# Hybrid encoder layer on one core: sums of w_ada row by row across the chunk ahead, in two alternating sums, and late transposes of x moved back

## The chip, the core and the metric

The program runs on one core of a Trainium2 chip. Five engines work side by side, each through its own queue in order: TensorE (PE: matmuls and transposes into PSUM), VectorE (DVE) and ScalarE (ACT) for elementwise work, GpSimd (POOL), and SyncE (SP), which here issues nearly all DMAs. The metric is the device time of one execution in microseconds (us), lower is better.

## What is computed

```
mod = silu(c) @ w_ada + b_ada                       # c: (1, 2048), w_ada: (2048, 3 * 2048)
shift, scale, gate = split(mod, 3)
h = rms_norm(x, g) * (1 + scale) + shift            # x: (1, 512, 2048)
q_a, k_a, v_a, z_a, q_r, k_r, v_r, z_r = split(h @ w_in)   # w_in: (2048, 7168)
y_a = dilated_attention_mixture(q_a, k_a, v_a)      # 8 heads of 128
y_r = bidirectional_retention(q_r, k_r, v_r)        # 4 heads
out = concat(y_a * silu(z_a), y_r * silu(z_r)) @ w_out     # w_out: (2048, 2048)
result = rms_norm(x + gate * out, final_gain)
```

All is float32. The change lies in how shift and scale are made and turned into h, ahead of the product with w_in.

## The kernel before

The 2048 columns of x and h are 16 blocks of 128, turned so that the block stands on the partitions: `xT[k]` is block k of the normalised x, 128 x 512. Each block of h is kept as a high part `hh[k]` and a low part `hl[k]` in fp32r, each piece of a weight likewise as two halves of a tile `w`, and a product is three matmuls (`mm3`): high x high, high x low, low x high.

The first part of the product with w_in goes through 13 **units** (256 columns of w_in each: q, k, v, z of the head pairs, `ph1`), but not block by block for one unit at a time: it goes by **chunks** of blocks, `CHUNKS = [1, 2, 2, 3, 4, 4]`. Chunk 0 is block 0, chunk 1 blocks 1 and 2, chunk 2 blocks 3 and 4, chunk 3 blocks 5 to 7, chunk 4 blocks 8 to 11, chunk 5 blocks 12 to 15. In each chunk all 13 units are multiplied with that chunk's blocks. So PE can begin with block 0 while shift and scale of the later blocks are still being made. Two units keep their sums in PSUM (`pp`), the others have their partial products in banks `pw` (three banks in turn), which ACT copies (chunk 0) or DVE adds (later) into tiles `acc0` to `acc12` in SBUF. In chunk 2 five of these go by ACT into tiles `more` instead and are added later.

A unit's piece of weights is loaded (`raw`), ACT casts its high half (L180), DVE subtracts to get the low half (L185), and PE multiplies. Three tiles `w` are in use in turn, so ACT's cast for a piece waits until PE has done the piece three before.

Beside that run, for each chunk ahead, the pieces made by `ada_pieces`: loads of the shift and scale columns of w_ada for the chunk's blocks (`araw`, three buffers; one holds 4, 4, 2, 2, 2 rows of blocks for chunks 1 to 5), and for each of the 16 blocks of rows one operation that multiplies it with the block's column of silu(c) and adds it into `aacc` (the first is an ACT activation at L239, the other 15 are DVE operations at L243, 512, 512, 768, 1024 and 1024 wide). Then `sums`: the sum of `aacc` over the partitions, for chunk 1 by matmuls with a column of ones (L257), for the others by transposes into the one bank of the pool `psM` (`psm`, L273), which ACT reads with accumulation (L278); for chunks 3 and later in two halves, one bank each in turn. Three small DVE operations make `sv` and `av`. Last `h_pieces`: ACT makes `hh` and `ht` (for chunk 1 DVE makes `ht`), DVE subtracts to get `hl` (L211).

What sets the order: the main loop feeds the units' pieces as **items**. An item is loaded when it is fed, converted `lead` items later (2 in chunk 0, 8 from then on) and multiplied two items after that. A table `agenda` holds what is to be called after which item: `plan` lays the pieces for the next chunk evenly over the items of the present one, from the third on, and the last quarter of x (row tile 3: transposes L380 and copies L391) after items 10 to 13. Since the items are loaded ten ahead of their matmuls, what is called at an item stands ahead of matmuls of ten items earlier. A scheduler then sets the final order of each engine by what it takes to be ready, except where `pin` keeps the order; `after` adds an order between two instructions without a semaphore.

Of the kernel before, what the change touches and what calls it, by code (L numbers as in the profile page):

```python
# [55 lines left out]
def trunk_kernel(ctx, tc, x, c, norm_gain, w_ada, b_ada, w_in, w_out, dec_f, dec_b, final_gain, out):  # L56
# [116 lines left out]
    def conv(src, n, at, pin_low=None):  # L173
# [7 lines left out]
        if pin_low is not None:  # L181
            pin_low.append(lambda: pin(nc.vector.tensor_tensor(dl, src, f32(dh), op=ALU.subtract)))
# [35 lines left out]
    def ada_pieces(k0, nk):  # L218
# [16 lines left out]
        def add(kr):  # L235
            rv = raws[kr]
            for a in range(npc):
                if kr + a == 0:
                    first = nc.scalar.activation(acc[:, :, :n], rv[:, a], AF.Copy, scale=ct[:, 0:1])  # L239
                    if k0 in (1, 3):  # L240
                        after(first, marks["hh"])
                else:
# [4 lines left out]
                    if k0 in (1, 3) and kr + a == 1:
                        after(ins, marks["hl"])

        def sums():  # L250
            ks = slice(k0, k0 + nk)
            sl = slice(NK + k0, NK + k0 + nk)
            if k0 == 1:
                ps = bank(psM, "psm")
                for b in range(2):
                    for j in range(nk):
                        nc.tensor.matmul(  # L257
                            ps[:, b * nk + j : b * nk + j + 1], acc[:, b, j * P : (j + 1) * P], ones[:, 0:1],
                            start=b + j == 0, stop=b + j == nk, skip_group_check=True,
                        )  # L260
# [1 line left out]
                nc.vector.tensor_tensor(av[:, ks], ps[:, nk : 2 * nk], bg[:, sl], op=ALU.add)
                marks["hl"] = nc.vector.tensor_tensor(
                    av[:, ks], av[:, ks], bg[:, 32 + k0 : 32 + k0 + nk], op=ALU.mult
                )
# [1118 lines left out]
```

## Time and profile before

| | us |
|---|---|
| median of 3 runs (lowest, highest) | 940.17 (938.87, 942.82) |
| the profiled execution | 940.26 |
| its span, first to last instruction | 938.5 |
| PE busy in it | 920.0 |
| DVE busy | 619.9 |
| ACT busy | 381.0 |
| mean granted TensorE clock | 0.997 |

The span is that of the instructions; 1.8 us of the execution's time lie around it. Busy time of PE is the union of the matmuls as they are shown, and these overlap: a matmul is shown for longer than it holds up the next one. So a stretch is judged by the number of its matmuls and by their step from start to start. A digit of the slices stands for 23.5 us, a fortieth of the span.

### The profile page before, as it was taken

The numbers are of one execution on the slowest core, as the hardware profiler recorded it, in microseconds if no ns is written. First come the engines' busy times: TensorE is split into PE (matmuls) and PEld (weight loads), VectorE is DVE, ScalarE is ACT, GpSimd is POOL, SyncE is SP. The second block draws the span as 40 slices with busy tenths as digits, with TensorE's granted clock in tenths as the row PEclk, the third lists the DMA queues.
The fourth block names the chain that finished last, engine by engine and source line by source line (L and its number), as shares of the span: only waits on it lengthen the run. The fifth ranks groups of instructions, "written<-read, shape, count | busy, mean of one in ns | idle before, by whom it ended". The sixth has DMA issues, their size and how long they took to land.

```text
span 938.5 us, 14336 instructions
## 1 busy us (share of the span) xinstructions
PE 920.0 (98%) x5578; PEld 807.9 (86%) x5578; DVE 619.9 (66%) x1096; ACT 381.0 (41%) x752; POOL 13.7 (1%) x25
## 2 busy tenths in 40 slices
PE   8999999999999999999999999999999999999996
PEld 5787788888988888988998899998899988888896
DVE  4899999959467886666675565845744382546554
ACT  4843525253254655444343232422343372324321
POOL 2000000000000000000000000000000000000001
PEclk9999999999999999999999999999999999999998
DMA  9987988524322222214444534434513148234305
GB/s 329 352 294 259 308 288 281 177 90 127 100 90 67 70 67 70 66 55 136 149 134 146 179 102 158 144 126 158 167 58 112 65 162 290 90 130 140 111 3 180
DMA packets 110244, 141.50 MB, mean 151 GB/s; under 512 B 5800, under 2 KB 81496, under 8 KB 109792
## 3 DMA queue, kind: packets, MB, share of 16 engines
q1 hardware_dynamic: 109072, 137.27, 44.6%
q10 hardware_dynamic: 1008, 3.28, 0.9%
q8 instruction: 44, 0.72, 0.3%
q14 instruction: 24, 0.20, 0.1%
q0 software_dynamic: 96, 0.03, 0.0%
HBM read 136.36 MB, written 4.20 MB: 150 GB/s over the span
## 4 chain that ended last, share of the span: by engine, by line
PE 84%; DVE 7%; DMA 4%; issue 2%; ACT 2%; POOL 0%; SPq 0%; POOLq 0%; DVEq 0%; ACTq 0%
PE pp L97 24%; PE pw L97 12%; PE pp L95 12%; PE po L97 12%; PE pw L95 6%; PE po L95 6%; DVE aacc L243 3%; PE op L97 3%; DMA araw<-in_w_ada_dram 2%; PE sp L97 2%; PE op L95 2%; PE tp L799 1%; DMA raw<-in_w_ada_dram 1%; DVE w L185 1%; PE sp L95 1%
## 5 line engine op out<-in xcount | busy, mean ns | idle before, releaser
L185 DVE TENSOR_TENSOR w<-raw,w 128x512 fp32r<-128x512 f32 (+1 forms) x288 | 193.6, 673 | 214.8 <-ACT w L180 214.5
L180 ACT CAST w<-raw 128x512 fp32r<-128x512 f32 (+1 forms) x289 | 174.7, 606 | 390.5 <-PE pp L97 187.1
L95 PE MATMUL pp<-w,hh 128*128 128x256 f32 x576 | 160.2, 278 | 0.0
L97 PE MATMUL pp<-w,hh 128*128 128x256 f32 x576 | 159.7, 277 | 0.0
L97 PE MATMUL pp<-w,hl 128*128 128x256 f32 x576 | 159.7, 277 | 0.0
L95 PEld LDWEIGHTS pp<-w,hh 128*128 128x128 f32 x576 | 108.4, 188 | 1.0 <-issue 0.2
L97 PEld LDWEIGHTS pp<-w,hh 128*128 128x128 f32 x576 | 108.3, 188 | 0.9
L97 PEld LDWEIGHTS pp<-w,hl 128*128 128x128 f32 x576 | 108.2, 188 | 0.0
L95 PE MATMUL pw<-hh,w 128*128 128x512 f32 x256 | 101.5, 397 | 3.4 <-DVE acc L994 2.1
L95 PE MATMUL pp<-hh,w 128*128 128x512 f32 x256 | 99.8, 392 | 0.4 <-DVE kl L699 0.4
L97 PE MATMUL pw<-hh,w 128*128 128x512 f32 x256 | 100.0, 391 | 0.1
L97 PE MATMUL pp<-hl,w 128*128 128x512 f32 x256 | 100.0, 391 | 0.0
L97 PE MATMUL pp<-hh,w 128*128 128x512 f32 x256 | 99.9, 390 | 0.0
L97 PE MATMUL pw<-hl,w 128*128 128x512 f32 x256 | 99.7, 391 | 0.0
L97 PE MATMUL po<-w,yh 128*128 128x512 f32 (+1 forms) x252 | 91.1, 361 | 0.0
L95 PE MATMUL po<-w,yh 128*128 128x512 f32 (+1 forms) x252 | 91.0, 361 | 0.0
L97 PE MATMUL po<-w,yl 128*128 128x512 f32 (+1 forms) x252 | 91.0, 361 | 0.0
L243 DVE SCALAR_TENSOR_TENSOR aacc<-araw,ct,aacc 128x512 f32<-128x512 f32 (+2 forms) x75 | 76.4, 1018 | 5.6 <-DMA araw<-in_w_ada_dram 2.9
L994 DVE TENSOR_TENSOR acc<-acc,pw 128x512 f32<-128x512 f32 x95 | 63.5, 686 | 4.6 <-PE pw L97 4.1
L95 PEld LDWEIGHTS pw<-hh,w 128*128 128x128 f32 x256 | 48.1, 188 | 17.2 <-DVE acc L994 4.7
L95 PEld LDWEIGHTS pp<-hh,w 128*128 128x128 f32 x256 | 48.0, 188 | 10.8 <-DVE kl L699 0.8
L97 PEld LDWEIGHTS pw<-hh,w 128*128 128x128 f32 x256 | 48.1, 188 | 10.6 <-DVE w L185 0.5
(237 smaller groups left out, 1568.6 us busy)
## 6 DMA issues: line engine op xcount, KB each, us to landing
raw<-in_w_in_dram SPq DMA_DIRECT2D x94, 512.0 KB, 3.6
araw<-in_w_ada_dram SPq DMA_DIRECT2D x48, 512.0 KB, 6.8
graw<-in_w_ada_dram SPq DMA_DIRECT2D x64, 256.0 KB, 3.0
raw<-in_w_out_dram SPq DMA_DIRECT2D x32, 512.0 KB, 3.7
raw<-in_w_in_dram SPq DMA_DIRECT2D x16, 384.0 KB, 4.1
araw<-in_w_ada_dram SPq DMA_DIRECT2D x16, 384.0 KB, 4.3
res<-in_x_dram SPq DMA_DIRECT2D x16, 256.0 KB, 6.2
raw<-in_w_in_dram SPq DMA_DIRECT2D x11, 256.0 KB, 5.1
```

The costliest lines, as they stand in the source:

```text
L95: nc.tensor.matmul(o, lh, rh, start=start, stop=False, skip_group_check=True)
L97: nc.tensor.matmul(o, a, b, start=False, stop=stop and b is (rl if swap else rh), skip_group_check=True)
L180: c1 = nc.scalar.copy(dh, src)
L185: c2 = nc.vector.tensor_tensor(dl, src, f32(dh), op=ALU.subtract)
L243: ins = nc.vector.scalar_tensor_tensor(acc[:, :, :n], rv[:, a], ct[:, kr + a : kr + a + 1], acc[:, :, :n], op0=ALU.mult, op1=ALU.add,)
L799: nc.tensor.transpose(tp_[:, j * P : (j + 1) * P], pt[:, j * P : (j + 1) * P], ident)
L994: nc.vector.tensor_tensor(accs[u][i], accs[u][i], ps[i], op=ALU.add)
```

## The change

Line numbers move by 2 to 42; the rows of the changed order carry the new ones (cast L182, low half L191, row add L254, transposed sums L290, reading L295, `hh` L203, `ht` L208, `hl` L217, add into `acc` L1033).

- The rows of w_ada are added one by one as separate pieces (`row`), not four or two in a piece. For chunks 2, 3 and 4 they are laid over the first 0.78, 0.78 and 0.62 of the items of the chunk before, counted from where PE is (`fed + LEAD1 + LOOK`) and not from where the loads are; the sums follow 0.04 of the items later and the making of h is spread up to 0.92, 0.92 and 0.78. Chunk 1 has places of its own in a table, chunk 5 is laid as before.
- For chunks 1 and 2 even and odd rows go into two sums, both begun by ACT. For chunk 1 the column matmuls take both sums (eight instead of four), for chunk 2 one DVE operation joins them ahead of the transposes. For chunk 1 `av` is made by one operation for each block, ahead of `sv`.
- Each row's add has an order after a conversion (`marks`).
- The last quarter of x is turned after items 10, 23, 25 and 27, and ACT alone copies it to `xT`.
- The larger lead of 8 begins two items later.

```diff
+LATE = 10, 23, 25, 27
+FIRST_AT = 3, 4, 5, 6, 8, 10, 13, 14, 15, 15, 16, 16
...
+        two = 2 * n <= 4 * P
+        part = [acc[:, :, :n], acc[:, :, n : 2 * n]] if two else [acc[:, :, :n]]
...
-        def add(kr):
+        def add(kr, only=None):
             rv = raws[kr]
-            for a in range(npc):
-                if kr + a == 0:
-                    first = nc.scalar.activation(acc[:, :, :n], rv[:, a], AF.Copy, scale=ct[:, 0:1])
+            for a in range(npc) if only is None else [only]:
+                r = kr + a
+                s = part[r % len(part)]
+                if r < len(part):
+                    first = nc.scalar.activation(s, rv[:, a], AF.Copy, scale=ct[:, r : r + 1])
...
+                    after(ins, marks["split" if k0 == 1 else "prev"])
...
+            if two:
+                nc.vector.tensor_tensor(part[0], part[0], part[1], op=ALU.add)
...
+        def row(r):
+            add(krs[r // npc], r % npc)
+            if r % npc == npc - 1 and r // npc + AR < len(krs):
+                load(krs[r // npc + AR])
...
+        if ends:
+            n_items, rows_end, h_end = ends
+            at = [i - 5 for i in range(AR)] + [r * rows_end * n_items / NK - 0.5 for r in range(NK)]
...
+            s = (rows_end + 0.04) * n_items
+            at += [s] + [s + 0.3 + (h_end * n_items - s) * j / len(hs) for j in range(len(hs))]
+            return list(zip(at, fs + [sums] + hs))
...
-        evacuated(3, b, dve if b else act, True)
+        evacuated(3, b, act, True)
...
+        if fed == NU + LEAD0:
+            early["lead"] = LEAD1
...
+            ends = {1: (0.78, 0.92), 2: (0.78, 0.92), 3: (0.62, 0.78)}.get(ci)
...
+            if ci == 0 or ends:
+                for at, f in nxt:
+                    agenda.setdefault(at if ci == 0 else fed + LEAD1 + LOOK + math.floor(at), []).append(f)
+            else:
+                plan(nxt, fed + LAG, span)
```

What this does to the order of the instructions, at the places that the prediction speaks of:

DVE, around the low halves `hl3` of chunk 2's blocks 3 and 4, in before (`w` are conversions of weights, `acc` the units' sums, `aacc` the sum of rows of w_ada, here that of chunk 3, 768 wide):

```order
L185 TENSOR_TENSOR w_866<-raw_637,w_866 128x512
L994 TENSOR_TENSOR acc11_0_365<-acc11_0_365,pw_869 128x512
L243 SCALAR_TENSOR_TENSOR aacc_750<-araw_860,ct_142,aacc_750 128x2x384
L994 TENSOR_TENSOR acc11_1_366<-acc11_1_366,pw_870 128x512
L211 TENSOR_TENSOR hl3_784<-ht_715,hh3_79 128x512
L211 TENSOR_TENSOR hl3_784<-ht_747,hh4_80 128x512
L185 TENSOR_TENSOR w_890<-raw1_665,w_890 128x512
L994 TENSOR_TENSOR acc4_0_351<-acc4_0_351,pw_893 128x512
L994 TENSOR_TENSOR acc4_1_352<-acc4_1_352,pw_894 128x512
L243 SCALAR_TENSOR_TENSOR aacc_750<-araw_863,ct_142,aacc_750 128x2x384
L185 TENSOR_TENSOR w_921<-raw_698,w_921 128x512
```

The same place in the changed order:

```order
L299 TENSOR_TENSOR av_144<-av_144,bg_147 128x2
L1033 TENSOR_TENSOR acc5_1_354<-acc5_1_354,pw_954 128x512
L217 TENSOR_TENSOR hl3_972<-ht_942,hh3_79 128x512
L217 TENSOR_TENSOR hl3_972<-ht_969,hh4_80 128x512
L191 TENSOR_TENSOR w_977<-raw1_713,w_977 128x512
L191 TENSOR_TENSOR w_995<-raw_786,w_995 128x512
L1033 TENSOR_TENSOR acc9_0_361<-acc9_0_361,pw_980 128x512
L254 SCALAR_TENSOR_TENSOR aacc_712<-araw_878,ct_142,aacc_712 128x2x384
L1033 TENSOR_TENSOR acc9_1_362<-acc9_1_362,pw_981 128x512
L254 SCALAR_TENSOR_TENSOR aacc_712<-araw_903,ct_142,aacc_712 128x2x384
L191 TENSOR_TENSOR w_1019<-raw1_813,w_1019 128x512
```

The `hl3` stood ahead of the conversion `w_890`, the eleventh of chunk 1, with a row for chunk 3 already ahead of it; now it stands behind all conversions of chunk 1, and the rows for chunk 3 begin behind it.

ACT, from the reading of the second three transposed blocks for chunk 3 (`psm`, `md` collects the sums) to the next conversions, in before:

```order
L278 ACTIVATE junk_1053,md_146<-psm_1047 128x128
L278 ACTIVATE junk_1055,md_146<-psm_1047 128x128
L990 COPY more4_0_1154<-pw_1140 128x512
L990 COPY more4_1_1156<-pw_1141 128x512
L180 CAST w_1161<-raw1_919 128x512
L197 ACTIVATE hh5_81<-xT3_94,sv_145,av_144 128x512
L202 ACTIVATE ht_1083<-xT3_94,sv_145,av_144 128x512
L197 ACTIVATE hh6_82<-xT3_94,sv_145,av_144 128x512
L202 ACTIVATE ht_1107<-xT3_94,sv_145,av_144 128x512
L197 ACTIVATE hh7_83<-xT3_94,sv_145,av_144 128x512
L202 ACTIVATE ht_1132<-xT3_94,sv_145,av_144 128x512
L180 CAST w_1181<-raw_969 128x512
```

The same place in the changed order:

```order
L295 ACTIVATE junk_1304,md_146<-psm_1300 128x128
L295 ACTIVATE junk_1306,md_146<-psm_1300 128x128
L295 ACTIVATE junk_1308,md_146<-psm_1300 128x128
L182 CAST w_1345<-raw_1071 128x256
L203 ACTIVATE hh5_81<-xT3_94,sv_145,av_144 128x512
L208 ACTIVATE ht_1313<-xT3_94,sv_145,av_144 128x512
L203 ACTIVATE hh6_82<-xT3_94,sv_145,av_144 128x512
L208 ACTIVATE ht_1336<-xT3_94,sv_145,av_144 128x512
L203 ACTIVATE hh7_83<-xT3_94,sv_145,av_144 128x512
L208 ACTIVATE ht_1339<-xT3_94,sv_145,av_144 128x512
L182 CAST w_1364<-raw1_1119 128x512
```

The six activations that make `hh` and `ht` stood ahead of the conversion `w_1181`, a piece of chunk 2 with four more of that chunk behind it; now they stand directly behind the reading and ahead of `w_1364`, a piece of chunk 3 itself.

PE, where chunk 3 begins, in before (`pp_343` and `pp_344` are the two banks of one unit, `pp_345` is the first of another):

```order
L97 MATMUL pp_344<-hh3_79,w_1300 128x512
L95 MATMUL pp_344<-hh4_80,w_1300 128x512
L97 MATMUL pp_344<-hl3_784,w_1300 128x512
L97 MATMUL pp_344<-hh4_80,w_1300 128x512
L95 MATMUL pp_343<-hh5_81,w_1331 128x512
L97 MATMUL pp_343<-hl5_1135,w_1331 128x512
L97 MATMUL pp_343<-hh5_81,w_1331 128x512
L95 MATMUL pp_343<-hh6_82,w_1331 128x512
L97 MATMUL pp_343<-hl5_1135,w_1331 128x512
```

The same place in the changed order:

```order
L97 MATMUL pp_344<-hh4_80,w_1261 128x512
L99 MATMUL pp_344<-hl3_972,w_1261 128x512
L99 MATMUL pp_344<-hh4_80,w_1261 128x512
L97 MATMUL pp_343<-hh5_81,w_1321 128x512
L97 MATMUL pp_344<-hh5_81,w_1321 128x512
L97 MATMUL pp_345<-hh5_81,w_1364 128x512
L99 MATMUL pp_343<-hl5_1342,w_1321 128x512
L99 MATMUL pp_343<-hh5_81,w_1321 128x512
L97 MATMUL pp_343<-hh6_82,w_1321 128x512
```

Before, chunk 3 began with all six matmuls of a piece one after another; now it begins with one matmul of `hh5` for each of three banks, the third with the weights `w_1364`, and the ones with `hl5` follow.

## Rows read from the trace of the kernel before

**Rows 1.** The page's slices: busy tenths of DVE in 40 equal slices.

```profile
DVE  4899999959467886666675565845744382546554
```

**Rows 2.** Table by stretches: stretch, length, busy us by engine, clock, DMA share, GB/s.

```profile
24.00:44.00 20.00, 19.45 (x105) 15.99 (x104) 17.61 (x31) 18.15 (x39) 0.00 (x0) 1.00 1.09 351
47.60:160.00 112.40, 107.77 (x597) 90.90 (x596) 106.30 (x156) 48.30 (x106) 0.00 (x0) 1.00 0.87 294
160.00:200.00 40.00, 40.00 (x180) 33.06 (x179) 34.84 (x51) 10.06 (x19) 0.00 (x0) 1.00 0.44 141
```

**Rows 3.** Groups of matmuls by shape, 47.6 to 160 us: count | busy, mean ns | idle.

```profile
L95 PE MATMUL pw<-hh,w 128*128 128x512 f32 x79 | 31.8, 402 | 2.8 <-DVE acc L994 2.1 <-ACT more L990 0.7
...
L95 PE MATMUL pw<-w,hh 128*128 128x256 f32 x84 | 23.8, 283 | 0.0
...
L97 PE MATMUL pp<-hl,w 128*128 128x512 f32 x28 | 10.9, 390 | 0.0
```

**Rows 4.** Timeline of PE: start, us, instruction; two steady stretches and one wait.

```profile
39.84 0.28 PE L95 MATMUL pw<-w,hh 128*128 128x256 f32 x1
...
41.43 0.28 PE L97 MATMUL pw<-w,hl 128*128 128x256 f32 x1
...
63.23 0.40 PE L97 MATMUL pw<-hh,w 128*128 128x512 f32 x1
64.34 0.50 PE L95 MATMUL pw<-hh,w 128*128 128x512 f32 x1 [0.71 <-DVE acc L994]
...
169.72 0.39 PE L97 MATMUL pw<-hh,w 128*128 128x512 f32 x1
...
171.08 0.39 PE L97 MATMUL pw<-hh,w 128*128 128x512 f32 x1
```

**Rows 5.** Waits of PE, 47 to 160 us: total us, times, longest.

```profile
PE pw L95 <- DVE acc L994: 2.1, 4, 0.7
PE psm L273 <- ACT junk L278: 1.5, 1, 1.5
```

**Rows 6.** Timeline of PE between chunk 0 and chunk 1.

```profile
44.59 1.05 PE L257 MATMUL psm<-ones,aacc 128*128 128x1 f32 x8 [0.15 <-DVE aacc L243]
46.05 0.52 PE L380 MATMUL psx<-ident,xt 128*128 128x128 f32 x3 [0.41 <-DVE av L262]
...
47.64 0.94 PE L95 MATMUL pp<-hh,w 128*128 128x512 f32 x3
```

**Rows 7.** Timeline of DVE in chunk 1.

```profile
55.53 3.10 DVE L243 SCALAR_TENSOR_TENSOR aacc<-araw,ct,aacc 128x512 f32<-128x512 f32 x4
58.55 0.68 DVE L185 TENSOR_TENSOR w<-raw,w 128x512 fp32r<-128x512 f32 x1
59.16 0.74 DVE L243 SCALAR_TENSOR_TENSOR aacc<-araw,ct,aacc 128x512 f32<-128x512 f32 x1
59.82 0.68 DVE L994 TENSOR_TENSOR acc<-acc,pw 128x512 f32<-128x512 f32 x1
60.42 0.75 DVE L243 SCALAR_TENSOR_TENSOR aacc<-araw,ct,aacc 128x512 f32<-128x512 f32 x1
...
77.53 1.02 DVE L243 SCALAR_TENSOR_TENSOR aacc<-araw,ct,aacc 128x768 f32<-128x768 f32 x1
78.46 1.29 DVE L994 TENSOR_TENSOR acc<-acc,pw 128x512 f32<-128x512 f32 x2
```

**Rows 8.** Timeline of ACT: start of a sum, readings, then activations up to a conversion.

```profile
29.64 0.72 ACT L239 ACTIVATE aacc<-araw,ct 128x512 f32<-128x512 f32 x1
...
101.27 0.26 ACT L278 ACTIVATE junk<-psm 128x128 f32<-128x128 f32 x1
...
101.52 0.27 ACT L278 ACTIVATE junk<-psm 128x128 f32<-128x128 f32 x1
...
105.62 0.82 ACT L197 ACTIVATE hh<-xT,sv,av 128x512 fp32r<-128x512 f32 x1
...
109.87 1.13 ACT L180 CAST w<-raw 128x512 fp32r<-128x512 f32 x2
```

More of the change, by code (lines that the diff above doesn't have):

```diff
@@ L181, in conv, with low @@
         if pin_low is not None:
[L182 removed]
+            def low():
+                marks["split"] = pin(nc.vector.tensor_tensor(dl, src, f32(dh), op=ALU.subtract))
+            pin_low.append(low)
             pin(c1)
@@ L243, in add @@
                     ins = nc.vector.scalar_tensor_tensor(
-                        acc[:, :, :n], rv[:, a], ct[:, kr + a : kr + a + 1], acc[:, :, :n],
-                        op0=ALU.mult, op1=ALU.add,
-                    )
-                    if k0 in (1, 3) and kr + a == 1:
+                        s, rv[:, a], ct[:, r : r + 1], s, op0=ALU.mult, op1=ALU.add
+                    )
+                    after(ins, marks["split" if k0 == 1 else "prev"])
+                    if k0 in (1, 3) and r == len(part):
                         after(ins, marks["hl"])
@@ L254, in sums @@
                 ps = bank(psM, "psm")
[L255 to L260, printed above, removed]
+                for i, s in enumerate(part):
+                    for b in range(2):
+                        for j in range(nk):
+                            nc.tensor.matmul(
+                                ps[:, b * nk + j : b * nk + j + 1], s[:, b, j * P : (j + 1) * P], ones[:, 0:1],
+                                start=i + b + j == 0, stop=i == len(part) - 1 and b + j == nk, skip_group_check=True,
+                            )
+                for j in range(nk):
+                    k = k0 + j
+                    marks["hl"] = nc.vector.tensor_scalar(
+                        av[:, k : k + 1], ps[:, nk + j : nk + j + 1], bg[:, NK + k : NK + k + 1],
+                        bg[:, 32 + k : 33 + k], op0=ALU.add, op1=ALU.mult,
+                    )
                 nc.vector.tensor_tensor(sv[:, ks], ps[:, 0:nk], bg[:, ks], op=ALU.add)
[L262 to L265, printed above, removed]
                 return
+            if two:
+                nc.vector.tensor_tensor(part[0], part[0], part[1], op=ALU.add)
             for b in range(2):
@@ L284, in ada_pieces @@
         krs = list(range(0, NK, npc))
+        if k0 == 1:
+            fs = [lambda i=i: load(krs[i]) for i in range(AR)] + [lambda: (add(krs[0]), load(krs[3]))]
+            fs += [lambda i=i: add(krs[i]) for i in (1, 2, 3)] + [sums] + h_pieces(k0, nk)
+            return list(zip(FIRST_AT, fs))
+        def row(r):
[5 more added lines that the diff above has]
+            at = [i - 5 for i in range(AR)] + [r * rows_end * n_items / NK - 0.5 for r in range(NK)]
+            fs = [lambda i=i: load(krs[i]) for i in range(AR)] + [lambda r=r: row(r) for r in range(NK)]
+            hs = h_pieces(k0, nk)
+            s = (rows_end + 0.04) * n_items
+            at += [s] + [s + 0.3 + (h_end * n_items - s) * j / len(hs) for j in range(len(hs))]
+            return list(zip(at, fs + [sums] + hs))
         def step(i):
@@ L919, in trunk_kernel @@
     fed = 0
-    for i, f in enumerate(late):
-        agenda.setdefault(LEAD1 + LOOK + i, []).append(f)
+    for at, f in zip(LATE, late):
+        agenda.setdefault(at, []).append(f)
     def plan(fs, start, span):
```

11 lines of the change are left out of this document (4 added, 7 removed).

## The prediction

> **The bound.** I read the page's slices first, then the table by stretches, then counted matmuls, and only then looked at waits. TensorE (PE) is full nearly everywhere; VectorE (DVE) is full only in the first fifth of the span, slices 3 to 9 [rows 1]. From 160 to 200 us PE is busy without a gap, and from 47.6 to 160 us DVE is at work 106.3 of 112.4 us [rows 2]. A busy PE says little, since a matmul is shown with 0.39 us while the next starts 0.23 us after it, so I count. In the stretch from 47.6 to 160 there are 320 matmuls of 512 columns (x79, 79, 78 and three times 28), 252 of 256 columns (three times x84) [rows 3] and 25 transposes. The steps from start to start are 1.36 us for 6, so 0.227, and 1.59 us for 14, so 0.114 [rows 4]; I put a transpose at 0.10. 72.6 + 28.7 + 2.5 = 103.8 us of work in 112.4: **8.6 us are lost there**. A wait costs more than its entry: after the one at 63.23 the first matmul takes 0.50 instead of 0.39, so 0.11 is added for starting again [rows 4]. The entries name the cause: PE waits for a PSUM bank that DVE has still to add into `acc`, four times, and once 1.5 us for the one bank in which the transposed sums lie [rows 5]. Just ahead of this stretch, between the last matmul of chunk 0 (it ends at 44.3) and the first of chunk 1 (47.64), lie eight passes of sums and seven transposes, 0.9 + 0.7 us, and about **1.7 us of idle PE** [rows 6]. After 160 us the kernel has nothing that this change touches but the entry into chunk 5, and behind that all five engines run the same instructions in the same order. The pot is thus 10.3 us, and no more.
>
> **Why DVE is full.** Its steps, start to start: conversion of a 512-column piece 0.61, an add of a row of w_ada at width 512 0.66 between other work, but 3.02 us for four in a row, 0.755 each, an `acc` add 0.60, a row at width 768 0.93 [rows 7]; width 1024 by the same slope 1.20. In before, DVE does the rows for chunk 2 and most of those for chunk 3 while PE is in chunk 1: the `hl3` subtraction stands behind 10 of chunk 1's 13 conversions, and the 768-wide rows of chunk 3 follow at once. In after it stands behind all 13. Between the `hl` of one chunk and the next the changed order has, for chunk 1, 12 conversions, 18 `acc` adds, 14 rows, one joining add, two `hl` and small ones: 7.3 + 10.8 + 9.2 + 0.6 + 1.5 = 29.4 us, against 13 units x 2.73 + 15 transposes = 37.1 us of PE. For chunk 2: 11 conversions, 15 `acc` adds and 15 rows of 0.93 up to the sum, 6.7 + 9.0 + 14.0 = 29.7, against 30.0 of PE up to its transposes. For chunk 3: 23 conversions, 21 adds, 14 rows of 1.20, 40 to 41 against 42. DVE fits everywhere, in chunk 2 by a hair, so the waits for `acc` go. I leave 0.3 us for chunk 2, where one bank comes free late by my count. Rows of chunk 5, which before shared chunk 3, now stand in chunk 4 (71 us of PE, 48 of DVE). That is the gain: 8.6 us minus what comes instead.
>
> **What comes instead: the sums are now due when they are ready.** From the finished sum to the first matmul of a chunk runs a chain over three engines: transposes on PE, one reading activation each on ScalarE (ACT) at 0.25, three small DVE operations of about 0.5 together, then two activations of 0.71 for each k, the six at 105.62 taking 4.25 [rows 8]. Before, it was covered by 16 us of matmuls at chunk 2, 23.6 at chunk 3 and 35 at chunk 4. In after what stands between the last transpose and the first matmul that needs the chain is 19, 18 and 30 matmuls: 4.3, 4.1 and 6.8 us.
> Into chunk 3, from the end of the eleventh unit: ACT converts `w_1321` first (to 0.65) and reads three blocks to 1.4; PE has five matmuls from 0.33 to 1.47, the second three transposes take the same bank, to 1.83; read by 2.7, `av` by 3.2, six activations to 7.5, and only then, on the same queue, the conversion of `w_1364`, to 8.1. PE has 16 matmuls and the two of `hh5` to 5.9, and then stands at `pp_345<-hh5,w_1364`: **2.3 us**. In before `w_1181` stands at the same place on ACT, and PE had other weights for 23 us.
> Into chunk 4: first reads to 1.65, second transposes to 2.24, reads to 3.4, `av` 4.0, eight activations to 9.8, `w_1848` to 10.35; PE reaches it at 9.05: 1.3, and 0.2 more for `w_1886` two conversions on: **1.5 us**. Into chunk 2: 6.3 against 6.35, **0.1**. Into chunk 5, whose sums are planned as before but are done later by a fuller queue: 11.0 against 10.4, **0.6**. With the 0.3 above 4.8 us, and six restarts of 0.11, 5.5 us. Bounds: if ACT serves the weights in time, 1.5; if DVE comes 1 us late to each of the four sums, 9.5, for there each us now passes straight to PE.
>
> **Chunk 0 and the transposes of x.** The order sets the sums between the last matmuls of chunk 0, and six matmuls behind them, 1.4 us, cover the way to `hh1`: most of the 1.7 us of idle go. Against that: the second sum doubles the column matmuls, four instructions in eight passes before, eight in sixteen now, +0.9; its start is one more activation of 0.72 [rows 8] on ACT, which is at work 18.15 of 20 us there [rows 2] and hands the banks of chunk 0 back, +0.65 at most; and DVE has rows in fours ahead of a conversion, whose low half I find about 1.2 us late for PE. What DVE saves there (one add of a row, and three copies of x that go to ACT) lies beside this. I take zero, first matmul of chunk 1 at 47.6 again; ends -1.5 and +1.5. Of the last 15 transposes four were still to do then, now ten: **+0.65**. No transpose is added, and ACT has room for the copies: it is at work 48.3 of 112.4 us from there on [rows 2].
> A rule that speaks against two alternating sums: here four dependent adds in a row took 0.755 each and one between others 0.66 [rows 7], so a dependent neighbour costs 0.10, and 13 such neighbours in chunks 0 and 1 cost 1.3 us of DVE. The Trainium skill (VectorE: DVE Perf Modes, The DRAIN you can't avoid) has it that after each operation the pipe is emptied before the next starts, whatever they share, so that only their number counts. By that the alternation saves nothing, and the time would be about 1 us longer, 938.7, by way of the late conversion in chunk 0. The rows differ from it, and I go by them.
>
> **Sum.** The profiled execution took 940.26 (span 938.5), the median is 940.17. 940.2 - 8.6 + 5.5 + 0.65 = **937.7 us**.
>
> **Rivals.** (A) *The chains stay covered*: ACT is quicker through them than by my count or PE reaches them later, and chunk 0 keeps its 1.7: 940.2 - 8.6 - 1.5 + 1.5 + 0.65 and 0.7 of restarts = 933. For: DVE is nearly done with chunk 4's rows 10 us before the transposes. Against: ACT's queue is in order, and the conversion stands behind the activations.
> (B) *DVE stays the bound*: in chunk 2 it has 29.7 us of work for 30.0; with waits in its queue it comes 1 us late to every sum, 5.5 becomes 9.5: 941 to 942, still no change that counts.
> (C) *Slower, by the loads*: the rows for chunks 3 and 4 are fetched later and more densely. Chunk 3's 16 rows of 0.39 MB and the weights beside them are 9.0 MB in 27.7 us, 323 GB/s; chunk 4's with weights 11.3 MB in 30, 376. From 24 to 44 us 351 GB/s were moved, from 47.6 to 160 a mean of 294 [rows 2]. At 351 the first fits and the second comes 2 us late to a sum with 10 us to spare; at 294 they are 2.8 and 8.4 us late, and DVE, waiting in order, holds conversions back: some 8 us more, 946. It decides from the point at which DVE's waits for `araw` pass 7 us in all; in before they are small.
> (D) *It does not do what it says*: ACT or the scheduler undoes the spreading. The orders show that it does.
>
> **Chances.** Forecast 0.58 (935.6 to 940.5), A 0.22 (933), B 0.11 (941.5), C 0.08 (946), D 0.01. Half a per cent, 4.7 us, is about what a measurement of this kernel can tell from no change. Faster by more: A and a tail of the forecast, 0.26; slower by more, from 944.9: C, 0.09; within: 0.65. The range takes in A in its better half and B: 933.0 to 942.0.
>
> **What would show it.** PE's waits on `acc` between 60 and 100 us gone; the matmul count from 47.6 to the entry into chunk 4 leaving 5 to 6 us lost, not 8.6; one PE wait of some 2 us for ACT's `w` at the first `hh5` matmuls and one of some 1.5 at `hh8`; the granted clock 1.00 as now. The column sums of chunk 1 as x16. I am wrong if DVE waits for `araw` by more than a few us, if PE waits at a sum for DVE's `aacc`, or if chunk 1 starts later than 49 or before 46 us.

## The result and the profile after

| | before | changed |
|---|---|---|
| median, us (lowest, highest) | 940.02 (938.87, 942.82) | 948.48 (947.85, 948.95) |
| ratio, 95% interval | 1 | 1.0085 [1.0062, 1.0108] |
| span of the profiled execution | 938.5 | 947.2 |
| busy: PE, DVE, ACT | 920.0, 619.9, 381.0 | 924.5, 616.2, 383.7 |
| mean granted clock | 0.997 | 0.996 |

The change makes the kernel about 8 us slower. The forecast was 937.7 us, its range 933.0 to 942.0.

The stretches of [rows 2] in the changed kernel, with 50 us more behind them (columns as there):

```profile
24.00:44.00 20.00, 18.88 (x102) 15.03 (x100) 16.51 (x29) 18.00 (x39) 0.00 (x0) 1.00 1.09 351
47.86:160.00 112.14, 109.22 (x601) 93.58 (x601) 97.31 (x145) 43.77 (x88) 0.00 (x0) 0.98 0.78 255
160.00:200.00 40.00, 38.49 (x171) 30.53 (x170) 31.17 (x48) 16.29 (x40) 0.00 (x0) 1.00 0.52 173
200.00:250.00 50.00, 45.33 (x252) 36.93 (x251) 41.09 (x63) 19.05 (x44) 0.88 (x1) 1.00 0.47 154
```

From 47.86 to 160 us PE is busier than before (a little of it at a lower clock, 0.98) and DVE has nine us less to do; that is the gain that was forecast. But from 160 to 250 us, where PE had no gap before, 6.2 us of PE are missing. PE's waits in the changed kernel, first from 47 to 160 us (the answer to [rows 5]), then from 160 to 260:

```profile
PE pp L97 <- ACT w L182: 2.2, 1, 2.2
PE pw L97 <- ACT more L1029: 0.7, 1, 0.7
...
PE pw L97 <- DVE acc L1033: 3.7, 4, 1.9
PE pw L97 <- ACT w L182: 1.2, 1, 1.2
PE pw L99 <- DVE w L191: 0.9, 2, 0.6
```

The waits for `acc` have not gone: three of the four stood between 63 and 83 us, and four now stand between 204 and 243.

To put a price on each place I add, over all matmuls, what the step to the next one is above the usual step of its form (0.227 us at 512 columns, 0.114 at 256), by stretches. This **start-to-start loss** counts stops, restarts and matmuls at a lower clock alike; each number is worked out from all matmul starts of one trace.

| us lost | 20-60 | 60-120 | 120-140 | 140-180 | 180-220 | 220-260 | whole span |
|---|---|---|---|---|---|---|---|
| before | 3.8 | 6.7 | 0.2 | 1.7 | 0.2 | 0.5 | 19.5 |
| changed | 4.1 | 1.8 | 4.3 | 0.4 | 6.7 | 3.5 | 27.2 |

27.2 - 19.5 = 7.7, and eight more column passes, 0.8 us (from 43.56 to 44.36 in the lines below), make 8.5 of the 8.7 us between the two spans. So nearly the whole difference lies between 20 and 260 us. A second trace of the changed kernel (f4 in the table further on) differs from this one by 0.7 us in the column 180-220 and by 1.6 in 220-260, so a single column is not good to better than that. The entry into chunk 4, at 181.8 and 184.8 us, holds 1.4 + 0.4 of the 6.7; the other places follow.

**Chunk 0 to chunk 1.** PE's timeline there, the answer to [rows 6]:

```profile
43.56 0.95 PE L270 MATMUL psm<-ones,aacc 128*128 128x1 f32 x8
...
44.91 0.95 PE L270 MATMUL psm<-ones,aacc 128*128 128x1 f32 x8
...
47.86 0.73 PE L97 MATMUL pp<-hh,w 128*128 128x512 f32 x2
```

Matmuls of chunk 0 fill the way between the passes, and chunk 1 begins at 47.86 instead of 47.64 us.

**Into chunk 3.** PE's timeline at its first matmuls, then three short stretches with the granted clock (the last column but two):

```profile
123.31 0.61 PE L97 MATMUL pp<-hh,w 128*128 128x512 f32 x2
126.13 0.50 PE L97 MATMUL pp<-hh,w 128*128 128x512 f32 x1 [2.21 <-ACT w L182]
126.47 0.40 PE L99 MATMUL pp<-hl,w 128*128 128x512 f32 x1
126.70 0.48 PE L99 MATMUL pp<-hh,w 128*128 128x512 f32 x1
126.98 0.63 PE L97 MATMUL pp<-hh,w 128*128 128x512 f32 x1
127.40 0.63 PE L99 MATMUL pp<-hl,w 128*128 128x512 f32 x1
127.83 0.63 PE L99 MATMUL pp<-hh,w 128*128 128x512 f32 x1
```

```profile
124.00:126.00 2.00, 0.00 (x0) 0.00 (x0) 0.40 (x1) 2.00 (x4) 0.00 (x0) 1.00 0.87 289
126.00:128.00 2.00, 1.87 (x6) 1.52 (x7) 2.00 (x4) 0.08 (x1) 0.00 (x0) 0.72 0.84 305
128.00:130.00 2.00, 2.00 (x7) 1.54 (x6) 1.29 (x2) 0.00 (x0) 0.00 (x0) 0.50 0.13 50
```

The wait is the one forecast, 2.2 us behind six activations on ACT. Behind it stands something that was not: the granted clock falls to 0.50, the lower of its two levels (1.2 GHz), and eight matmuls step by 0.43 instead of 0.23 us, 1.6 us more.

**In chunk 4.** DVE's timeline there, and three stretches around it:

```profile
201.35 0.69 DVE L191 TENSOR_TENSOR w<-raw,w 128x512 fp32r<-128x512 f32 x1
201.95 1.28 DVE L254 SCALAR_TENSOR_TENSOR aacc<-araw,ct,aacc 128x1024 f32<-128x1024 f32 x1
203.15 0.68 DVE L191 TENSOR_TENSOR w<-raw,w 128x512 fp32r<-128x512 f32 x1
203.75 1.28 DVE L254 SCALAR_TENSOR_TENSOR aacc<-araw,ct,aacc 128x1024 f32<-128x1024 f32 x1
204.95 0.68 DVE L1033 TENSOR_TENSOR acc<-acc,pw 128x512 f32<-128x512 f32 x1
```

```profile
190.00:200.00 10.00, 9.95 (x45) 7.90 (x44) 9.75 (x12) 2.16 (x4) 0.00 (x0) 1.00 0.96 330
200.00:210.00 10.00, 8.52 (x34) 5.81 (x33) 9.85 (x11) 2.18 (x4) 0.00 (x0) 1.00 1.00 348
210.00:220.00 10.00, 9.28 (x44) 6.81 (x43) 8.09 (x14) 4.82 (x20) 0.00 (x0) 1.00 0.36 108
```

Nearly every second operation of DVE is a row of chunk 5. The 15 rows stand between 186.5 and 214.0 us, with 8 conversions and 7 `acc` adds: 18.0 + 4.9 + 4.2 = 27.1 us of DVE in a time for which PE has 8 pieces, 8 x 2.73 = 21.8 us. In before the same 15 rows lay between 140.6 and 189 us, most of them in chunk 3.

**At 234 us.** ACT's timeline, the issue of the load that it stands at, and PE behind it:

```profile
228.50 0.62 ACT L182 CAST w<-raw 128x512 fp32r<-128x512 f32 x1 [2.58 <-PE pw L99]
234.74 0.21 ACT L575 ACTIVATE e<-dec 128x8 f32<-128x8 f32 x1 [5.62 <-DMA raw<-in_w_in_dram]
234.85 0.60 ACT L182 CAST w<-raw 128x512 fp32r<-128x512 f32 x1
```

```profile
228.56 0.43 SPq L571 DMA_DIRECT2D dec<-n_ret_decay_logit_b_dram  x1
```

```profile
236.83 0.38 PE L97 MATMUL pw<-w,hh 128*128 128x256 f32 x1 [1.92 <-DVE acc L1033]
```

Sums and h of chunk 5 are late behind these rows, so the small loads that may only follow them are late (`dec` is issued at 228.6 us, before at 215.3), ACT stands in its order at `e<-dec`, and the conversion behind it is late; DVE, in its order, stands at that piece's low half until 235.5 us, and PE waits for the `acc` add behind it (1.92 us). Before, ACT waited 0.82 us at this place. (The profile names a load of weights as the releaser, which `e<-dec` does not read; in the second trace of this kernel it names `dec`.)

### The profile page after: what moved, and what is told of

It is laid out like the page before. It is cut to its first block, busy times and chain, and to the rows that moved or that the text cites. A ratio compares the mean times of both kernels' runs of the same rounds, so it can differ in the third digit from the quotient of the medians.

```text
span 947.2 us, 14353 instructions
## 1 busy us (share of the span) xinstructions
PE 924.5 (98%) x5586; PEld 808.6 (85%) x5586; DVE 616.2 (65%) x1092; ACT 383.7 (41%) x757; POOL 12.5 (1%) x25
## 4 chain that ended last, share of the span: by engine, by line
PE 84%; DMA 5%; DVE 5%; ACT 3%; issue 1%; SPq 1%; POOL 0%; POOLq 0%; DVEq 0%; ACTq 0%
PE pp L99 26%; PE pp L97 13%; PE pw L99 13%; PE po L99 10%; PE pw L97 7%; PE po L97 5%; PE op L99 3%; PE sp L99 2%; DMA araw<-in_w_ada_dram 2%; PE op L97 2%; PE tp L836 1%; DMA raw<-in_w_out_dram 1%; SPq L125 1%; PE sp L97 1%; DVE w L191 1%
## 5 line engine op out<-in xcount | busy, mean ns | idle before, releaser
L191 DVE TENSOR_TENSOR w<-raw,w 128x512 fp32r<-128x512 f32 (+1 forms) x288 | 193.0, 671 | 216.9 <-ACT w L182 216.8
L182 ACT CAST w<-raw 128x512 fp32r<-128x512 f32 (+1 forms) x289 | 174.2, 606 | 391.8 <-PE pp L99 179.7
L254 DVE SCALAR_TENSOR_TENSOR aacc<-araw,ct,aacc 128x1024 f32<-128x1024 f32 (+2 forms) x73 | 73.4, 1019 | 3.0 <-ACT aacc L250 2.6
L1033 DVE TENSOR_TENSOR acc<-acc,pw 128x512 f32<-128x512 f32 x95 | 62.8, 680 | 6.8 <-PE pw L99 6.5
```

The costliest lines, as they stand in the source:

```text
L182: c1 = nc.scalar.copy(dh, src)
L254: ins = nc.vector.scalar_tensor_tensor(s, rv[:, a], ct[:, r : r + 1], s, op0=ALU.mult, op1=ALU.add)
L1033: nc.vector.tensor_tensor(accs[u][i], accs[u][i], ps[i], op=ALU.add)
```

## The experiments

The theory has two parts. First, the order that each row now has after a conversion (`after(ins, marks[...])`) holds also the rows of chunk 5, whose places in the agenda the change left alone. Before, the scheduler drew them forward into chunk 3; now it can't, and they stand where they were written, two to a piece, at the start of chunk 4. Second, there is the wait into chunk 3 with the clock behind it. Rivals: the late h of chunk 4 takes DVE's lead away (*late entry*); the loads set the pace (*transfers*); two sums or the moved transposes cost something.

Start-to-start loss (one trace each) and ratio to the kernel before (all executions), for all runs:

| | 20-60 | 60-120 | 120-140 | 140-180 | 180-220 | 220-260 | ratio [95%] |
|---|---|---|---|---|---|---|---|
| before | 3.8 | 6.7 | 0.2 | 1.7 | 0.2 | 0.5 | 1 |
| changed | 4.1 | 1.8 | 4.3 | 0.4 | 6.7 | 3.5 | 1.0085 [1.0062, 1.0108] |
| e1_order5_alone | 3.8 | 5.5 | 0.2 | 0.3 | 2.4 | 1.5 | 1.0028 [1.0017, 1.0040] |
| e2_spread5 | 4.3 | 1.8 | 2.7 | 0.4 | 2.1 | 4.2 | 1.0050 [1.0031, 1.0069] |
| e3_free5 | 4.1 | 1.8 | 4.3 | 0.5 | 4.7 | 0.5 | 1.0029 [1.0016, 1.0043] |
| e4_c4_as_before | 4.2 | 2.0 | 7.9 | 1.8 | 0.2 | 0.6 | 1.0036 [1.0023, 1.0049] |
| e5_early3 | 4.3 | 1.8 | 0.8 | 2.2 | 4.8 | 2.1 | 1.0057 [1.0043, 1.0071] |
| e6_early34_free5 | 4.2 | 2.3 | 1.4 | 4.1 | 0.2 | 0.3 | 1.0003 [0.9993, 1.0012] |
| e7_one_sum | 6.1 | 1.7 | 2.9 | 0.4 | 6.2 | 2.2 | 1.0077 [1.0064, 1.0091] |
| e8_late_old | 4.7 | 1.8 | 2.7 | 0.4 | 6.5 | 2.1 | 1.0082 [1.0068, 1.0095] |
| f1_early3_c4_before | 4.4 | 2.0 | 1.2 | 6.1 | 0.2 | 0.8 | 1.0029 [1.0018, 1.0040] |
| f2_same_one_sum | 4.7 | 2.2 | 1.3 | 5.2 | 0.2 | 0.5 | 1.0034 [1.0023, 1.0044] |
| f3_off4 | 4.0 | 2.8 | 0.8 | 4.3 | 0.2 | 0.4 | 1.0000 [0.9990, 1.0011] |
| f4_after_again | 4.0 | 1.9 | 4.2 | 0.4 | 7.4 | 1.9 | 1.0081 [1.0058, 1.0104] |

### The order of chunk 5's rows

Alone, put into the kernel before:

```diff
+                    if k0 == 12:
+                        after(ins, marks["prev"])
```

> The kernel before with one edit: each of the 15 row adds of chunk 5 (1024 wide) is ordered after the conversion that stood ahead of it when it was written, as in the changed kernel; nothing else is touched. Theory: this order alone keeps the scheduler from drawing the rows forward into chunk 3, so that they stand in pairs between the first conversions of chunk 4, 15 of 1.20 us within some 26 us, where DVE then has more to do than PE; PE waits for acc and for late weights there, and the kernel becomes 4 to 7 us slower than before (944 to 947), with the acc waits of before still at 60 to 100 us. Rival (late entry): the loss in chunk 4 came from h of blocks 8 to 11 being ready only as PE needs it, which took DVE's lead away; here that h is early as in before, so under 1.5 us slower (941.5 at most).

Measured: 942.78 us, ratio 1.0028, 2.6 us slower. The rows moved as expected, and from 180 to 260 us the loss rose from 0.7 to 3.9. The stretch that answers to the changed kernel's:

```profile
200.00:210.00 10.00, 8.82 (x42) 6.77 (x42) 8.67 (x13) 3.53 (x19) 0.00 (x0) 1.00 0.46 151
```

But from 60 to 180 us 2.6 us of loss went, since DVE has fewer rows in chunks 2 and 3. So the mechanism shows without any late h, against the rival, and its net price here is under my lower bound: part of what the rows cost in chunk 4 they had cost in chunk 3. The profiled execution took 940.67 us, the fastest of seven: its trace shows 3.2 us lost and 2.6 gained, and where the other executions lost the rest of the median's 2.6 us no trace shows.

Taken out of the changed kernel:

```diff
-                    after(ins, marks["split" if k0 == 1 else "prev"])
+                    if k0 < 12:
+                        after(ins, marks["split" if k0 == 1 else "prev"])
```

> The changed kernel without the order after a conversion for the rows of chunk 5 alone; its places in the agenda are unchanged. Theory: the scheduler draws a part of the rows forward to the end of chunk 3, the others stay dense in the first half of chunk 4, so a part of the loss is given back: 2 to 5 us faster than the changed kernel, 943.5 to 946.5. Rival (late entry): the loss is that of the late h of chunk 4, so no change, 948.

Measured: ratio 1.0029 against 1.0085, 5.3 us faster, though h of chunk 4 is as late as before this edit. The late-entry rival falls. From 192 to 260 us no loss above that of before is left; the stop at 234 us has gone as well. What is left at the entry is a new wait, since three of the freed rows now stand ahead of the low halves on DVE, and with it a fall of the clock: 4.4 us lost there instead of 1.8. The 5.3 us net and these 2.6 make 7.9, which is what the columns 180-260 of the changed kernel hold beyond its entry into chunk 4 and the kernel before. DVE's timeline, then two stretches:

```profile
180.86 3.92 DVE L254 SCALAR_TENSOR_TENSOR aacc<-araw,ct,aacc 128x1024 f32<-128x1024 f32 x3
184.70 2.49 DVE L217 TENSOR_TENSOR hl<-ht,hh 128x512 fp32r<-128x512 f32 x4
```

```profile
184.00:186.00 2.00, 0.57 (x2) 0.47 (x3) 2.00 (x4) 1.61 (x3) 0.00 (x0) 0.92 0.67 182
186.00:188.00 2.00, 2.00 (x7) 1.54 (x6) 2.00 (x4) 0.00 (x0) 0.00 (x0) 0.50 0.95 363
```

Density or transfers? With the same late h and the rows one to an item:

```diff
-            ends = {1: (0.78, 0.92), 2: (0.78, 0.92), 3: (0.62, 0.78)}.get(ci)
+            ends = {1: (0.78, 0.92), 2: (0.78, 0.92), 3: (0.62, 0.78), 4: (0.6, 0.7)}.get(ci)
...
-                    agenda.setdefault(at if ci == 0 else fed + LEAD1 + LOOK + math.floor(at), []).append(f)
+                    agenda.setdefault(at if ci == 0 else fed + (5 if before_last else LEAD1 + LOOK) + math.floor(at), []).append(f)
...
-                agenda.setdefault(fed + LAG + span, []).append(open_wk)
+                agenda.setdefault(fed + 24, []).append(open_wk)
```

> The changed kernel with the rows of chunk 5 added one by one, one for each item of chunk 4 from the fifth on, the sums after item 21 and h by item 23, and the tables after it four items later; all else as in the changed kernel. Theory: DVE has 2.4 us of work per item against PE's 2.73, so the waits for acc between 195 and 213 us go and with them most of the two later stops at 234 and 242 us: 5 to 7 us faster than the changed kernel, 941.5 to 943.5. The wait into chunk 3 (2.2 us, with the granted clock falling behind it) and into chunk 4 (1.2 us) stay. Rival (transfers): in 200 to 210 us the DMA engines were busy throughout; if the loads set the pace, the rows come no sooner and the gain is under 2 us, with DVE waiting for araw instead.

Measured: ratio 1.0050, 3.3 us faster than the changed kernel. The stretches:

```profile
200.00:210.00 10.00, 10.00 (x46) 8.29 (x45) 9.66 (x12) 1.88 (x4) 0.00 (x0) 1.00 0.94 322
210.00:220.00 10.00, 10.00 (x46) 8.29 (x45) 9.96 (x14) 2.49 (x4) 0.00 (x0) 1.00 0.43 148
230.00:240.00 10.00, 8.40 (x63) 7.81 (x62) 5.24 (x10) 7.55 (x13) 0.23 (x1) 0.92 0.05 12
```

From 200 to 220 us PE now has no gap, with 322 GB/s and DMA engines at 0.94; in the changed kernel DVE had been at work 9.85 of the 10 us from 200 on, and it waited for a row's load once, 0.4 us. So the density of the rows on DVE was the cause, not the transfers. (Of what this trace gained 1.6 us are the clock, which did not fall behind the wait into chunk 3 here.) The total was missed for the reason in the third line: the sums now come so late that the entry into chunk 5 has waits of its own, with a fall of the clock (0.92).

### Chunks 3 and 4

```diff
-            ends = {1: (0.78, 0.92), 2: (0.78, 0.92), 3: (0.62, 0.78)}.get(ci)
+            ends = {1: (0.78, 0.92), 2: (0.78, 0.92)}.get(ci)
```

and the order after a conversion for `k0 < 8` only:

> The changed kernel with chunk 4's rows, sums and h laid as in before, and no order after conversions for the rows of chunks 4 and 5; chunks 1 to 3 as changed. Theory: the losses from the entry into chunk 4 on go (1.8 us at the entry, about 7 between 195 and 245 us), the wait into chunk 3 and the clock's fall behind it stay; the rows of chunk 4 move back into chunk 3's first part: 7 to 9 us faster than the changed kernel, 939.5 to 941.5, the same as before. Rival: DVE, which the row order kept even, falls behind in chunk 3 and returns acc waits there: 944.

Measured: ratio 1.0036, 4.6 us faster than the changed kernel, not 7 to 9. From 180 us on all is as in before, but the entry into chunk 3 became worse, from 4.3 to 7.9 us, by another way than the rival's. On DVE a freed row of chunk 4 stands ahead of `av`, which comes at 122.45 instead of 121.03 us, and so ACT's six activations and the conversion behind them are later: PE waits 3.3 us for it instead of 2.2. Three more rows stand ahead of the low halves of chunk 3, 1.0 us more, and the lower clock lasts twice as long. DVE, and the stretch behind it:

```profile
124.71 3.94 DVE L254 SCALAR_TENSOR_TENSOR aacc<-araw,ct,aacc 128x1024 f32<-128x1024 f32 x3 [0.31 <-DMA araw<-in_w_ada_dram]
128.57 1.89 DVE L217 TENSOR_TENSOR hl<-ht,hh 128x512 fp32r<-128x512 f32 x3
```

```profile
130.00:134.00 4.00, 4.00 (x11) 3.12 (x10) 2.25 (x3) 0.02 (x1) 0.00 (x0) 0.50 0.91 292
```

Chunk 3 an item earlier, its rows behind the low halves of chunk 2 (`marks["low"]` is the last low half of h written so far):

```diff
-            ends = {1: (0.78, 0.92), 2: (0.78, 0.92), 3: (0.62, 0.78)}.get(ci)
+            ends = {1: (0.70, 0.84), 2: (0.78, 0.92), 3: (0.62, 0.78)}.get(ci)
...
-                    agenda.setdefault(at if ci == 0 else fed + LEAD1 + LOOK + math.floor(at), []).append(f)
+                    agenda.setdefault(at if ci == 0 else fed + LEAD1 + LOOK - {2: 1}.get(ci, 0) + math.floor(at), []).append(f)
...
+                    if k0 == 5:
+                        after(ins, marks["low"])
```

> The changed kernel with the sums for chunk 2 at 0.70 and 0.84 of the items, and the rows, sums and h for chunk 3 one item earlier, the first of these rows behind the low halves of chunk 2; chunks 4 and 5 as in the changed kernel. Theory: the wait of PE for the six activations ahead of chunk 3 goes (2.4 us), and with it the fall of the granted clock that stood right behind it (eight matmuls with 0.2 us each, 1.6 us), since the clock fell because PE stood: 4 us faster than the changed kernel, 944.5. Rival (clock falls by itself): the wait goes and the slow stretch stays, 946. Other rival (DVE has no room): rows an item earlier bring waits for acc back in chunks 1 and 2, no gain, 948.

Measured: ratio 1.0057, 2.6 us faster (3.5 by the medians). Into chunk 3 3.5 of the 4 us went, wait and slow clock together:

```profile
124.00:126.00 2.00, 1.79 (x9) 1.14 (x8) 2.00 (x5) 0.25 (x1) 0.00 (x0) 1.00 0.00 0
126.00:128.00 2.00, 2.00 (x10) 1.66 (x9) 2.00 (x4) 0.41 (x1) 0.00 (x0) 1.00 0.52 165
```

The 1.4 us at the entry into chunk 4 are still there, at 178.8 us and so in the column before, and chunk 5's rows still cost 4.4 us in chunk 4 (4.9 in the changed kernel); the column behind it is 2.1 instead of 3.5. Both edits together, with chunk 4 three items earlier:

```diff
-                    agenda.setdefault(at if ci == 0 else fed + LEAD1 + LOOK - {2: 1}.get(ci, 0) + math.floor(at), []).append(f)
+                    agenda.setdefault(at if ci == 0 else fed + LEAD1 + LOOK - {2: 1, 3: 3}.get(ci, 0) + math.floor(at), []).append(f)
...
+                    if k0 < 12:
```

> The run before this one, with two things more: rows, sums and h of chunk 4 three items earlier, and no order after a conversion for the rows of chunk 5. Theory: what was lost against the kernel before is now known place by place: the wait into chunk 3 with its slow matmuls (4.0), the wait for the low halves into chunk 4 with its slow matmuls (4.4 in the run that freed chunk 5's rows), the dense rows of chunk 5 (gone in that run). With all three gone, 943.0 - 4.0 - 4.4 = 934.6, faster than the kernel before by some 5.5 us, which are the acc waits of chunks 1 and 2 less 1 to 2 us at chunk 0. Rival: DVE, with rows for chunks 4 and 5 beside each other again, brings acc waits back in chunk 3, and it ends within 1 us of the kernel before, 939 to 941.

Measured: 940.28 us, ratio 1.0003 [0.9993, 1.0012]. The two edits take 5.3 and 2.6 us by themselves, 7.9 in all, and 7.7 together with the earlier chunk 4: in size they account for the loss. That earlier chunk 4 is not taken apart from them here, and the columns show both sides: 12.6 us less from 120 to 140 and 180 to 260, and 3.7 more from 140 to 180. So no gain is left, as the rival had it, though its place is only half the story. The stretches in chunk 3:

```profile
150.00:160.00 10.00, 8.43 (x38) 6.36 (x37) 8.34 (x13) 3.79 (x9) 0.00 (x0) 1.00 0.81 283
160.00:170.00 10.00, 8.59 (x40) 6.67 (x39) 9.76 (x16) 8.84 (x25) 0.00 (x0) 1.00 0.69 213
```

One wait is for `acc` (1.2 us), one for a conversion on ACT (1.4). With a fourth item:

```diff
-                    agenda.setdefault(at if ci == 0 else fed + LEAD1 + LOOK - {2: 1, 3: 3}.get(ci, 0) + math.floor(at), []).append(f)
+                    agenda.setdefault(at if ci == 0 else fed + LEAD1 + LOOK - {2: 1, 3: 4}.get(ci, 0) + math.floor(at), []).append(f)
```

> The run early34_free5 with rows, sums and h of chunk 4 four items earlier than in the changed kernel instead of three. In that run PE still waited 1.4 us for a converted weight at the entry into chunk 4. Theory: that wait goes, 1.5 us faster, a ratio of 0.999 to the kernel before. Rival: the two waits for acc near 151 us (1.9 us there) grow by as much, since the same rows stand in less time: no change, 1.000.

Measured: ratio 1.0000 [0.9990, 1.0011]. Neither had it right: the `acc` waits went and the wait for ACT grew to 1.9, since it has nothing to do with the entry. Eight activations of h in a row, 158.75 to 164.5 us, hold a conversion wherever they stand, and the clock fell behind it:

```profile
164.00:166.00 2.00, 0.93 (x3) 0.79 (x4) 2.00 (x4) 1.85 (x4) 0.00 (x0) 0.89 0.88 322
166.00:168.00 2.00, 2.00 (x5) 1.20 (x5) 2.00 (x5) 0.00 (x0) 0.00 (x0) 0.50 0.76 287
```

Activations laid between the conversions were not tried. No variant is faster than the kernel before; this one and e6 equal it.

Chunks 4 and 5 as in before, with chunk 3 an item earlier, and the same with one sum for chunk 1 (`two = k0 == 3`); the line that moves chunk 3 and `marks["low"]` are as above:

```diff
-            ends = {1: (0.78, 0.92), 2: (0.78, 0.92), 3: (0.62, 0.78)}.get(ci)
+            ends = {1: (0.70, 0.84), 2: (0.78, 0.92)}.get(ci)
...
+                    if k0 < 8:
                         after(ins, marks["split" if k0 == 1 else "prev"])
+                    if k0 in (5, 8):
+                        after(ins, marks["low"])
```

> The changed kernel with chunks 2 and 3 one item earlier (as in the run early3) and chunks 4 and 5 laid as in the kernel before, their rows without the order after a conversion, but chunk 4's rows behind the low halves of chunk 3. Theory: early3 still lost 1.8 us at the entry into chunk 4 and 5 us behind it to chunk 5's rows; with the old places both go: 944.9 - 1.8 - 5 = 938, a ratio of 0.998 to 0.999 against the kernel before. Rival: the rows of chunk 4, freed, now stand as densely in the first part of chunk 3 as chunk 5's did in chunk 4, and PE waits for acc there: 941 or more, a ratio of 1.002.

> The run before this one with one sum instead of two for chunk 1 alone (chunk 2 keeps two). In the run with one sum everywhere PE lost 1.2 us less from 20 to 40 us, 3.2 more from 40 to 60 (of it 1.2 at a lower granted clock behind a stop at the sums), and did eight passes fewer (0.9). Theory: 0 to 1 us slower than with two sums. Rival (a second start on ScalarE costs more than it brings): 1 us faster.

Measured: 1.0029 and 1.0034. The rival of the first was right: the rows of chunk 4, now behind the low halves, fill DVE and PE waits there.

```profile
140.00:150.00 10.00, 7.48 (x56) 6.35 (x54) 10.00 (x13) 2.05 (x4) 0.00 (x0) 1.00 0.96 323
```

It is the changed kernel's loss to chunk 5's rows, one chunk earlier. One sum or two makes no difference that the intervals show.

### Sums, transposes, and the kernel again

```diff
-        two = 2 * n <= 4 * P
+        two = False
```

> The changed kernel with one sum for chunks 1 and 2, as before: one start on ScalarE, 15 dependent row adds, four column matmuls, no joining add. By the prediction's rows (dependent neighbours cost 0.10 us each, 13 of them) DVE has 1.3 us more and the low halves in chunk 0 come later; eight passes fewer on PE and one activation of 0.72 less on ScalarE take 0.9 and up to 0.7 back: between 0.5 us faster and 1 us slower, 948 to 949.5. By the rule that only the number of operations counts: 0.9 us or more faster, 947.5 or less, with the row adds of chunk 1 at the same length from start to start as with two sums.

```diff
-LATE = 10, 23, 25, 27
+LATE = 10, 11, 12, 13
...
-        evacuated(3, b, act, True)
+        evacuated(3, b, dve if b else act, True)
```

> The changed kernel with the last quarter of x turned and copied as in the kernel before (after items 10 to 13, half of the copies on DVE). The prediction put this part at +0.65 us for six transposes behind the first matmul of chunk 1, with copies on ScalarE at nothing. From 20 to 40 us PE lost 3.1 us in the changed kernel against 2.0 before. Theory: ScalarE, at work 18 of 20 us there, hands the copies and banks back later; with the old places 0.5 to 1.5 us faster than the changed kernel, 947 to 948. Rival: the copies on DVE take its room in chunk 0 and it becomes 1 us slower.

Measured: 1.0077 and 1.0082, against 1.0085 and 1.0081 for the changed kernel: neither part weighs. In the trace one sum gives 1.2 us back from 20 to 40 us (no second start on ACT) and loses 3.2 from 40 to 60, where PE stands at the sums again and some 1.2 us of it are matmuls at half the granted clock. The rows of chunk 1 on DVE, four in turn on two sums in the changed kernel, then three in a row on one sum in this run:

```profile
34.27 2.73 DVE L254 SCALAR_TENSOR_TENSOR aacc<-araw,ct,aacc 128x512 f32<-128x512 f32 x4
...
35.57 2.32 DVE L254 SCALAR_TENSOR_TENSOR aacc<-araw,ct,aacc 128x512 f32<-128x512 f32 x3
```

With the last one taken at 0.75 the steps are (2.73 - 0.75) / 3 = 0.66 and (2.32 - 0.75) / 2 = 0.785. A dependent neighbour costs 0.125 us. The prediction had 0.10, since it divided three dependent steps and an ordinary one by four (3 x 0.785 + 0.66 = 3.02). The Trainium skill (VectorE: DVE Perf Modes, The DRAIN you can't avoid) has the next operation wait for an empty pipe after every operation; the same section adds that one which is not held starts earlier, which the prediction passed over. In these rows an independent add starts 0.66 us after one that is shown for 0.75, so before its end, and a dependent one does not. By the rule that only the number counts the two steps would be equal; the rows decide against it, while the whole time could not tell the two apart.

The changed kernel itself once more:

> The changed kernel itself once more, for the two losses that came and went between kernels which are the same there: behind the wait into chunk 3, of the same 2.37 us in five traces, eight matmuls at half the granted clock followed in two and none in three; and the stop at 234 us was 2.1 us in the changed kernel and 0.6 to 0.8 in three others with the same order. Theory: both belong to the execution, not to the order; one look more shows the 2.37 us again, and at least one of the two losses gone, with a span 1 to 3 us shorter. Rival: both are fixed by the order of this kernel, and the trace repeats with 947 us.

Measured: 948.11 us, span 946.9. The wait of 2.37 us came again and the clock fell again; the stop at 234 us was 0.7 instead of 2.1 (ACT at `e<-dec` 4.2 instead of 5.6 us), while in chunk 4 0.7 us more were lost. So the rival holds for the total.

## Why the prediction was wrong, point by point

- **The pot (8.6 us from 47.6 to 160).** Mostly right: from 60 to 120 us 4.9 of 6.7 us went and no wait for `acc` is left there. Of the pot 0.84 us were PE's wait for ACT's copy to `more`, which DVE's load does not touch; it stood at 90.9 us and now stands at 106.0, with the same loss. That part should not have been in the term.
- **DVE by chunks.** Chunks 1 to 3 fit, as worked out. The step that failed is the sentence behind: "Rows of chunk 5, which before shared chunk 3, now stand in chunk 4 (71 us of PE, 48 of DVE)". It compares sums over a whole chunk and puts the price of the move at nothing. The rows don't spread over the 71 us; they stand in the first 27.5 of them, where 27.1 us of DVE meet 21.8 of PE. The loss there is 6.7 less 1.8 at the entry, 4.9 us, and 3.0 more from 220 to 260 us, where what waits for chunk 5's sums is late: 7.9 us (7.0 in the second trace). The diff had the reason in one line, the order after a conversion for every row. The description of the change has chunk 5 "laid as before" and the prediction its sums "planned as before"; that is true of the agenda alone, and though the prediction saw that the rows had moved, it didn't ask where in the chunk they stand. For the same reason "After 160 us the kernel has nothing that this change touches but the entry into chunk 5" was wrong.
- **The new waits.** Into chunk 3 2.3 us were forecast, 2.2 and a loss of 2.37 measured; into chunk 4 1.5, and 1.4 + 0.4 measured, for the conversions named. Into chunk 2 nothing above 0.2; at the entry into chunk 5 none.
- **The clock.** "the granted clock 1.00 as now" failed, and the sum had no term for it: behind the wait into chunk 3 it was 0.50, 1.6 us. PE's stops in chunks 1 to 5 before had cost at most 1.6 us each and had shown no fall.
- **Chunk 0.** Zero was right as a total, in part by luck: chunk 1 begins 0.2 us later. ACT's second start, put at 0.65 us at most, costs 1.1 us from 20 to 40 us (with one sum they are gone), and the filled sums give 0.9 back from 40 to 60.
- **The sum.** -2.5 forecast; with 7.9 for chunk 5, 1.6 for the clock, 0.8 for `more`, 0.3 at the entry into chunk 4 and -0.6 at that into chunk 5 it is +7.5, and 8.0 (by the ratio) to 8.5 (by the medians) were measured. (The sum's 0.65 for the transposes of x stays in the -2.5; the run with their old places shows no difference.)
- **Rivals.** C (946) came near in time by a mechanism that isn't there: DVE waits for `araw` 0.4 us in all. B had the right engine and the wrong place. None of the signs under "I am wrong if" appeared, since all looked at the start of chunk 1, the loads and the sums and none at what the order does to the rows that were not re-laid. Of the signs of being right, the waits for `acc` between 60 and 100 us went, and two failed: the clock, and the 5 to 6 us that were to be left up to the entry into chunk 4. There 6.5 us are left from 60 to 180 us and 1.8 at the entry.

## What to carry to other kernels

An order between two instructions doesn't only keep one from running early; it takes from the scheduler the freedom to use a slack far ahead, so every user of the edited helper has to be looked up in the changed order, also those whose plan is unchanged. Compare the load of an engine over the stretch in which the work stands, not over the chunk in which it falls. And a stop of PE of some 2 us is to be costed with what the clock may add behind it, here 1.4 to 1.6 us in some executions and nothing in others.
